# Gate and up projections in other column pieces: 272+272, 512+32, 288+256 per weight block, 384+160

## The chip, the cores and the metric

The kernel runs on one core of a Trainium2 chip. The metric is the device time of one execution, in microseconds (us), as the median of several runs. TensorE is called PE below, its weight loads PEld; DVE is VectorE, ACT ScalarE, POOL GpSimd, SP the engine whose queue starts the weight transfers.

## What is computed

One decoder layer for 512 prompt tokens and 32 sample tokens, 544 in all, with a model width of 1024. A token mixer with three branches (pooling, stick-breaking attention, convolution) is followed by a layer norm and a SwiGLU feed forward, which is the part that matters here:

```python
def _ffn(x, wg, wu, wd):
    return (jax.nn.silu(x @ wg) * (x @ wu)) @ wd
...
xp = _layernorm(ALPHA * xp + _ffn(xp, ffn_w_gate[l], ffn_w_up[l], ffn_w_down[l]), ln2_g[l], ln2_b[l])
```

`wg` and `wu` are 1024 x 2816, `wd` is 2816 x 1024, all float32. Prompt and sample tokens go through the same weights.

## The kernel before, in words

Activations lie with their features on the 128 partitions and the 544 tokens along the free axis: `x1h` and `x1l` are [128, 8, 544], for 8 blocks of 128 features. Matmul operands are in a rounded format (F32R); to come near float32 accuracy each value is split in a high part and a low rest, for activations (`x1h`, `x1l`) and weights (`wh`, `wl`) alike. `gemm` (L212 to L224) then makes one product of three: for each of the 8 feature blocks k it runs wh times x1h, wh times x1l and wl times x1h, which is 24 matmuls into one PSUM bank (a tile of 128x512 float32). The weight block of 128x128 is the stationary operand; the token columns stream past. Every matmul instruction loads its own weights: the trace lists one weight load for each matmul.

The feed forward's first half has NF = 22 blocks f of 128 hidden features. Each has a gate block and an up block of 1024x128 weights. `ffn_half` (L899 to L909) takes one half of the tokens: `HALVES` is columns 0 to 288 (the 32 sample tokens and 256 prompt tokens) and 288 to 544. For a half it runs the gate's 24 matmuls into a bank, Silu on ACT from that bank into `sg` (L905), the up's 24 matmuls into another bank, the product with `sg` on DVE (L908), and the split of the result into `gh` (ACT, L209) and `gl` (DVE, L210). Blocks f = 0 and 1 have their weights ready early and run half by half; blocks 2 to 21 run half 0 and then half 1, so that PE sees gate 288, up 288, gate 256, up 256 columns, 24 matmuls each.

Weights come through `_Weights`: SP's queue brings two blocks of 128 columns at once as `raw`, and `prepare` makes `wh` (ACT, L131) and `wl` (DVE, L132), two blocks ahead, into a pool with three buffers of each. A buffer comes free with the last matmul that reads it. Banks for the results come from a pool of PSM = 5. The tile framework's scheduler places the instructions of each engine; around the change they stand in the order of the code. After the last block the down projection reads `gh` and `gl` as moving operands, in the same two halves.

Of the kernel before, what the change touches and what calls it, by code (L numbers as in the profile page):

```python
# [9 lines left out]
F32 = mybir.dt.float32  # L10
F32R = mybir.dt.float32r
I32 = mybir.dt.int32
AF = mybir.ActivationFunctionType
ALU = mybir.AluOpType
PSUM = bass.MemoryType.PSUM

P = 128
D = 1024
KD = D // P
# [4 lines left out]
T = NP + NS  # L24
# [16 lines left out]
TA = NS + PH  # L41
HALVES = ((0, TA), (TA, T))
# [104 lines left out]
def hybrid_layer_kernel(  # L147
# [6 lines left out]
    nc = tc.nc  # L154
# [13 lines left out]
    def bank(tag="mm"):  # L168
        return pst[tag].tile([P, 512], F32, tag=tag, name=tag)
# [37 lines left out]
    def split_psum(hi, lo, ps, scale=None):  # L207
        if scale is None:
            nc.scalar.copy(hi, ps)  # L209
            nc.vector.tensor_tensor(out=lo, in0=ps, in1=hi.bitcast(F32), op=ALU.subtract)  # L210
        else:
            nc.scalar.mul(hi, ps, scale)  # L212
            nc.vector.scalar_tensor_tensor(out=lo, in0=ps, scalar=scale, in1=hi.bitcast(F32), op0=ALU.mult, op1=ALU.subtract)

    def gemm(ps, wt, rt, kts, c0, c1, wc0=0, first=True, last=True, r0=0, r1_=P):
        n = c1 - c0
        wh, wl = wt
        rh, rl = rt
        steps = [(a, k) for k in range(len(kts)) for a in range(3)]
        for s, (a, k) in enumerate(steps):  # L220
            lw = (wh, wh, wl)[a][r0:r1_, k, wc0:wc0 + P]
            rr = (rh, rl, rh)[a][r0:r1_, kts[k], c0:c1]
            ins = nc.tensor.matmul(ps[:, :n], lw, rr, start=first and s == 0, stop=last and s == len(steps) - 1)  # L223
        return ins  # L224

    # constants
    vt = cp.tile([P, NV], F32, name="vt")
    et = cp.tile([P, NEARLY], F32, name="et")
    ident = et[:, E_ID:E_ID + P]
# [51 lines left out]
    def sqrt_set(ins):  # L281
        with tc.issue_after(ins):
            nc.scalar.preload_act_table_set("sqrt_and_others")
# [2 lines left out]
        with tc.issue_after(ins):  # L286
            nc.scalar.preload_act_table_set("natural_log_exp_and_others")

# [1 line left out]
    nc.gpsimd.memset(qbd, 0.0)  # L290
    nc.gpsimd.memset(osum, 0.0)
    with pool("s0", 1, reuse_waits="tile") as s0:
# [36 lines left out]
        nc.vector.scalar_tensor_tensor(out=pix, in0=pix, scalar=128.0, in1=rwc[:, 0:1].to_broadcast([P, 8 * DB]), op0=ALU.mult, op1=ALU.add)  # L329
        nc.vector.scalar_tensor_tensor(out=piv, in0=piv, scalar=32.0, in1=rwc[:, 1:2].to_broadcast([P, 2 * DB]), op0=ALU.mult, op1=ALU.add)  # L330

# [1 line left out]
    pps = ExitStack()  # L333
    pp = pps.enter_context(pool("pp", reuse_waits="tile"))
    ph_ = pp.tile([P, 2, T], F32R, name="ph")
# [7 lines left out]
    for c in range(2):  # L343
# [8 lines left out]
        n = PB + NP + DB * PEXT  # L352
# [11 lines left out]
        for s in range(2):  # L364
            r = slice(64 * s, 64 * s + 64)
            nc.vector.scalar_tensor_tensor(out=pf[r, NS + PB:], in0=sm[s][r, 2 * PB:PB + NP], scalar=ec_(E_IW + c, 1)[r],
                                           in1=ue[r, 2 * PB:PB + NP], op0=ALU.mult, op1=ALU.subtract)
            nc.vector.scalar_tensor_tensor(out=sview(pf[r, :NS], DS), in0=sview(sm[s][r, PB + NP:], PEXT)[:, :, PB:], scalar=ec_(E_IW + c, 1)[r],
                                           in1=uv[r, :, PB:], op0=ALU.mult, op1=ALU.subtract)
# [5 lines left out]
        nc.gpsimd.dma_start(pool_p[c * P:(c + 1) * P], ue[:, NP:NP + PB])  # L375
        nc.gpsimd.dma_start(pool_s[c * P:(c + 1) * P], fl)

# [1 line left out]
    av = []  # L379
    for c in range(2):  # L380
        a = s1.tile([P, T], F32, tag="av", bufs=2, name=f"av{c}")
# [3 lines left out]
    for c in range(2):  # L385
        sg = s1.tile([P, T], F32, tag="sg", bufs=2, name=f"sg{c}")
# [95 lines left out]
                    nc.vector.tensor_scalar(gt[:, m, c0:c1], ps[:, :c1 - c0], bias, None, op0=ALU.add)  # L482
        return gt, nc.scalar.activation(gt, gt, AF.Sigmoid)

# [1 line left out]
    def gate0(g):  # L486
        gt, ins = gates(0, g, mp_, "gt", GTB)
        for m in range(2):
            nc.vector.tensor_tensor(out=mg[:, 2 * g + m], in0=mg[:, 2 * g + m], in1=gt[:, m], op=ALU.mult)
        return ins  # L490

    pw = w.next()
    for mo in range(KD):
        g, m = mo // 2, mo % 2
        rs = 64 * (g % 2)
        for c0, c1 in HALVES:
            ps = bank("z")
            for n_, (a, b) in enumerate(((pw[0], ph_), (pw[0], pl_), (pw[1], ph_))):
                nc.tensor.matmul(ps[:, :c1 - c0], a[rs:rs + 64, g // 2, m * P:(m + 1) * P], b[rs:rs + 64, g // 2, c0:c1],  # L499
                                 start=n_ == 0, stop=n_ == 2)  # L500
# [4 lines left out]
    for g in range(NGA):  # L505
        ins = gate0(g)

# [1 line left out]
    def qkv_q(ap, hp):  # L509
        qh = ap.tile([P, NP], F32R, tag="qh", name=f"qh{hp}")  # L510
        ql = ap.tile([P, NP], F32R, tag="ql", name=f"ql{hp}")
        for hf, ps in enumerate(chunk_psums(w.next(), X, KX)):
            a = hf * PH
            split_psum(qh[:, a:a + PH], ql[:, a:a + PH], prompt_of(ps, hf), 0.125)
            for s in range(2 if hf == 0 else 0):
                r = slice(64 * s, 64 * s + 64)
                h = 2 * hp + s
                nc.scalar.mul(qbd[r, hp, :, DS * h:DS * h + DS], sview(ps[r, :NS], DS), 0.125)
        return qh, ql
# [89 lines left out]
                exp_set(conv_norm().ins)  # L609
    conv_st.close()  # L610

# [1 line left out]
    sam = ExitStack()  # L613
    sp = sam.enter_context(pool("sam", reuse_waits="tile"))
    g1s = ExitStack()
# [80 lines left out]
    for b in range(DB):  # L696
# [8 lines left out]
        for br, g in [c for c, n_ in zip(steps, at_batch) if n_ == b]:  # L705
# [3 lines left out]
            elif br == 3:  # L709
                cw_ = w.next()  # L710
                for m in range(2):
                    mo = 2 * g + m
                    for c0, c1 in HALVES:
                        ps = bank()
# [16 lines left out]
    cst_.close()  # L731
    s2c.close()

# [1 line left out]
    late = {}  # L735
    for g in range(2):
        w.group(big(w_out, g * 256, 0, KD, 256), KD, 256, ((0, 128), (128, 128)))
# [22 lines left out]
    for g in range(4):  # L760
# [7 lines left out]
        for m, hf in both:  # L768
                mo = 2 * g + m
                c0, c1 = HALVES[hf]  # L770
                ps = bank()
# [8 lines left out]
    pst["mm"] = ctx.enter_context(pool("mm2", PSM, space=PSUM, reuse_waits="tile"))  # L780
    pst["tp"] = ctx.enter_context(pool("tp2", 8 - PSM, space=PSUM, reuse_waits="tile"))

# [1 line left out]
    xp1 = ctx.enter_context(pool("x1", side="right", reuse_waits="tile"))  # L784
    x1h = xp1.tile([P, KD, T], F32R, name="x1h")
    x1l = xp1.tile([P, KD, T], F32R, name="x1l")
# [87 lines left out]
    for m in range(4):  # L874
        wt = w.next()
# [3 lines left out]
    first = [[w.next(), w.next()] for _ in range(2)]  # L879
# [10 lines left out]
    s6t.close()  # L890
    s6.close()

# [1 line left out]
    gp = ctx.enter_context(pool("gp", side="right", reuse_waits="tile"))  # L894
    gh = gp.tile([P, NF, T], F32R, name="gh")
    gl = gp.tile([P, NF, T], F32R, name="gl")
    X1 = (x1h, x1l)
    with pool("s7", 2, reuse_waits="tile") as s7:
        def ffn_half(f, hf, wt, sgs):  # L899
            c0, c1 = HALVES[hf]  # L900
            pg = bank()
            gemm(pg, wt[0], X1, KX, c0, c1)
            n = c1 - c0
            sg = s7.tile([P, TA], F32, tag="sg", bufs=4, name=f"sg{f}{hf}")[:, :n]
            lasts.append(nc.scalar.activation(sg, pg[:, :n], AF.Silu))  # L905
            pu = bank()
            gemm(pu, wt[1], X1, KX, c0, c1)
            nc.vector.tensor_tensor(out=sg, in0=pu[:, :n], in1=sg, op=ALU.mult)  # L908
            split_psum(gh[:, f, c0:c1], gl[:, f, c0:c1], sg)  # L909

        lasts = []
        for hf in range(2):
            for f in range(2):
                ffn_half(f, hf, first[f], None)
        for f in range(2, NF):
            wt = [w.next(), w.next()]
            for hf in range(2):
                ffn_half(f, hf, wt, None)
        sqrt_set(lasts[-1].ins)
    wp2s.close()  # L920

# [26 lines left out]
    for m in range(KD - 1):  # L948
        pss = [bank(), bank()]
        for j, (k0, k) in enumerate(pieces):  # L950
            wt = w.next()
# [124 lines left out]
```

## Time and profile before

| what | value |
|---|---|
| runs | 900.57 and 901.0 us, median 900.79 |
| profiled execution | span of 899.0 us from its first to its last instruction |
| median of the runs less the span | 1.8 us |
| mean granted clock of TensorE | 0.994 of full speed |

Busy times of engines are in the rows below. Matmuls are pipelined, and the duration of one contains its way through the array; what a matmul costs in a row of many is the distance from its start to the next one's, which is called its pitch here.

### The profile page before, as it was taken

Reading aid. Unit: us, or ns where it says so; the run is one execution under the profiler, and the core shown is the slowest. Engines: PE = TensorE matmul, PEld = TensorE weight load, DVE = VectorE, ACT = ScalarE, POOL = GpSimd, SP = SyncE. Lnnn points to the kernel's source line nnn. Section 1 sums busy time; section 2 is a strip of 40 time slices with the busy share of each in tenths; the row PEclk is TensorE's granted clock in tenths of the full one; section 3 lists DMA queues with packets and bytes.
Section 4 is the critical chain, followed back from the end, with each engine's and each line's share of the span. In section 5 each row is a group of like instructions: output and inputs, shape, how many; then the busy total and the mean of one; then the engine's idle time right before and its main releaser. Section 6 shows DMA issues by size and latency. Waiting matters only on the chain.

```text
span 899.0 us, 16259 instructions
## 1 busy us (share of the span) xinstructions
PE 877.0 (98%) x6889; PEld 811.0 (90%) x6889; DVE 478.1 (53%) x845; ACT 348.5 (39%) x583; POOL 134.8 (15%) x158
## 2 busy tenths in 40 slices
PE   7999999999999999999999999999999999999993
PEld 6999999887886667779999999999999999999993
DVE  4899886887343454449646433333333333334437
ACT  5445377776533315244513333232323232222211
POOL 1430100005257476310001000000000000000002
PEclk9999999999999999999999999999999999999997
DMA  9314323214648688646610122233232322323322
GB/s 291 118 34 115 96 73 113 65 38 137 214 143 289 238 290 291 229 136 225 207 48 1 48 68 76 92 95 94 94 95 94 95 58 73 101 75 83 96 81 100
DMA packets 96393, 110.36 MB, mean 123 GB/s; under 512 B 4416, under 2 KB 88224, under 8 KB 94144
## 3 DMA queue, kind: packets, MB, share of 16 engines
q1 hardware_dynamic: 87840, 73.12, 26.4%
q0 software_dynamic: 8480, 36.20, 11.9%
q8 instruction: 54, 0.88, 0.4%
q14 instruction: 19, 0.16, 0.1%
HBM read 104.44 MB, written 4.87 MB: 122 GB/s over the span
## 4 chain that ended last, share of the span: by engine, by line
PE 96%; DVE 2%; ACT 1%; DMA 1%; issue 0%; SPq 0%; another core or an unknown queue 0%; DVEq 0%; ACTq 0%
PE mm L223 82%; PE z L654 3%; PE o L680 2%; PE z L564 2%; PE o L586 2%; PE tp L583 1%; PE tp L795 1%; PE o L681 1%; PE z L499 1%; DMA raw<-in_w_in 1%; PE tp L861 1%; DVE y L999 0%; DVE y L991 0%; PE tp L687 0%; DVE rc L572 0%
## 5 line engine op out<-in xcount | busy, mean ns | idle before, releaser
L132 DVE TENSOR_TENSOR wl<-raw,wh 128x1024 fp32r<-128x1024 f32 (+1 forms) x129 | 152.3, 1184 | 137.7 <-ACT wh L131 136.5
L131 ACT CAST wh<-raw 128x1024 fp32r<-128x1024 f32 (+1 forms) x129 | 129.3, 1006 | 238.9 <-PE mm L223 212.2
L223 PE MATMUL mm<-xh,wh 128*128 128x256 f32 (+1 forms) x672 | 198.3, 295 | 5.7 <-ACT wh L131 5.6
L223 PE MATMUL mm<-x1l,wh 128*128 128x288 f32 (+1 forms) x704 | 202.7, 288 | 0.0
L223 PE MATMUL mm<-x1h,wl 128*128 128x288 f32 (+1 forms) x704 | 201.4, 287 | 0.0
L223 PE MATMUL mm<-x1h,wh 128*128 128x288 f32 (+1 forms) x704 | 200.5, 286 | 0.1
L223 PE MATMUL mm<-xl,wh 128*128 128x256 f32 (+1 forms) x672 | 198.1, 295 | 0.2 <-DVE xl L210 0.2
L223 PE MATMUL mm<-xh,wl 128*128 128x288 f32 (+1 forms) x672 | 197.0, 294 | 0.7 <-issue 0.7
L223 PEld LDWEIGHTS mm<-xh,wh 128*128 128x128 f32 x672 | 127.9, 191 | 16.9 <-issue 9.8
L223 PEld LDWEIGHTS mm<-xl,wh 128*128 128x128 f32 x672 | 127.8, 190 | 8.6 <-issue 7.3
L223 PEld LDWEIGHTS mm<-xh,wl 128*128 128x128 f32 x672 | 127.5, 190 | 8.6 <-issue 7.7
L223 PEld LDWEIGHTS mm<-x1l,wh 128*128 128x128 f32 x704 | 132.2, 188 | 0.2
L223 PEld LDWEIGHTS mm<-x1h,wh 128*128 128x128 f32 x704 | 132.0, 188 | 0.4 <-ACT sg L905 0.3
L223 PEld LDWEIGHTS mm<-x1h,wl 128*128 128x128 f32 x704 | 132.0, 188 | 0.0
L223 PE MATMUL mm<-gl,wh 128*128 128x256 f32 (+1 forms) x352 | 101.7, 289 | 0.0
L223 PE MATMUL mm<-gh,wh 128*128 128x256 f32 (+1 forms) x352 | 101.3, 288 | 0.0
L223 PE MATMUL mm<-gh,wl 128*128 128x256 f32 (+1 forms) x352 | 100.8, 286 | 0.0
L623 POOL DMA_INDIRECT kr<-in_ck,pix x64 | 67.6, 1056 | 44.7 <-PE z L654 20.6
L908 DVE TENSOR_TENSOR sg<-mm,sg 128x288 f32<-128x288 f32 (+1 forms) x44 | 19.4, 441 | 91.8 <-PE mm L223 91.8
L223 PEld LDWEIGHTS mm<-gl,wh 128*128 128x128 f32 x352 | 66.1, 188 | 0.1
L223 PEld LDWEIGHTS mm<-gh,wh 128*128 128x128 f32 x352 | 66.2, 188 | 0.0
L223 PEld LDWEIGHTS mm<-gh,wl 128*128 128x128 f32 x352 | 66.1, 188 | 0.0
(216 smaller groups left out, 1202.8 us busy)
## 6 DMA issues: line engine op xcount, KB each, us to landing
raw<-in_w_in SPq DMA_DIRECT2D x14, 1024.0 KB, 8.2
raw<-in_w_g SPq DMA_DIRECT2D x11, 1024.0 KB, 5.3
raw<-in_w_u SPq DMA_DIRECT2D x11, 1024.0 KB, 5.4
raw<-in_w_d SPq DMA_DIRECT2D x16, 512.0 KB, 4.0
raw<-in_w_in SPq DMA_DIRECT2D x12, 512.0 KB, 3.9
raw<-in_w_out SPq DMA_DIRECT2D x4, 1024.0 KB
raw<-in_w_d SPq DMA_DIRECT2D x8, 384.0 KB, 4.3
raw<-in_w_att_o SPq DMA_DIRECT2D x4, 512.0 KB, 3.4
```

What stands on the lines that cost most here:

```text
L131: self.nc.scalar.copy(hi[:, a:b], v[:, a:b])
L132: self.nc.vector.tensor_tensor(out=lo[:, a:b], in0=v[:, a:b], in1=hi[:, a:b].bitcast(F32), op=ALU.subtract)
L223: ins = nc.tensor.matmul(ps[:, :n], lw, rr, start=first and s == 0, stop=last and s == len(steps) - 1)
L499: nc.tensor.matmul(ps[:, :c1 - c0], a[rs:rs + 64, g // 2, m * P:(m + 1) * P], b[rs:rs + 64, g // 2, c0:c1], start=n_ == 0, stop=n_ == 2)
L564: nc.tensor.matmul(zp[:, :wd], a[r, qs], b[r, :wd], start=n_ == 0, stop=n_ == 2)
L583: nc.tensor.transpose(tp[:, kb], rc[:, s, kb * P:(kb + 1) * P], ident)
L586: nc.tensor.matmul(op_[64 * s:64 * s + 64, :P], vtok[:, kb, 64 * s:64 * s + 64], at[:, kb], start=kb == 0, stop=kb == i)
L623: nc.gpsimd.indirect_dma_start(out=kr[:, u].rearrange("p h c -> p (h c)"), out_offset=None, in_=ck, in_offset=bass.IndirectOffsetOnAxis(ap ...
L654: nc.tensor.matmul(zp[32 * jj:32 * jj + 32, :256], qbd[:, hp, b], kvt[b, "k", jj][:, :, hp], start=hp == 0, stop=hp == 3)
L680: nc.tensor.matmul(op_[32 * c:32 * c + 32], at[:, j], kvt[b, "v", j // 4][:, j % 4], start=j < 4, stop=j >= 4 and c < 3)
L681: nc.tensor.matmul(op_[96:128], at[96:128, 8], vs96[96:128], start=False, stop=True)
L908: nc.vector.tensor_tensor(out=sg, in0=pu[:, :n], in1=sg, op=ALU.mult)
```

## The change

It replaces `ffn_half` by a part with free column bounds, `ffn_part`, and by `ffn_both`, and chooses for each group of five blocks f how the tokens are cut: f = 2 to 6 as 272+272 columns, 7 to 11 as 512+32, 12 to 16 by `ffn_both`, 17 to 21 as 384+160. `ffn_both` keeps the pieces of 288 and 256 columns, but for each weight block k it runs both pieces with wh, each with x1h and x1l, then both with wl, into two banks at a time. Blocks 0 and 1 are as before. The `sg` tiles grow from 288 to 512 columns. The other changed lines of the diff are comments.

```diff
-        def ffn_half(f, hf, wt, sgs):
-            c0, c1 = HALVES[hf]
+        def piece(f, ps, c0, c1, act, sg=None):
+            n = c1 - c0
+            if act:
+                sg = s7.tile([P, 512], F32, tag="sg", bufs=4, name=f"sg{f}{c0}")[:, :n]
+                lasts.append(nc.scalar.activation(sg, ps[:, :n], AF.Silu))
+                return sg
+            nc.vector.tensor_tensor(out=sg, in0=ps[:, :n], in1=sg, op=ALU.mult)
+            split_psum(gh[:, f, c0:c1], gl[:, f, c0:c1], sg)
+
+        def ffn_part(f, cols, wt):
+            c0, c1 = cols
             pg = bank()
             gemm(pg, wt[0], X1, KX, c0, c1)
-            n = c1 - c0
-            sg = s7.tile([P, TA], F32, tag="sg", bufs=4, name=f"sg{f}{hf}")[:, :n]
-            lasts.append(nc.scalar.activation(sg, pg[:, :n], AF.Silu))
+            sg = piece(f, pg, c0, c1, True)
             pu = bank()
             gemm(pu, wt[1], X1, KX, c0, c1)
-            nc.vector.tensor_tensor(out=sg, in0=pu[:, :n], in1=sg, op=ALU.mult)
-            split_psum(gh[:, f, c0:c1], gl[:, f, c0:c1], sg)
+            piece(f, pu, c0, c1, False, sg)
+
+        def ffn_both(f, wt):
+            sg = [None, None]
+            for j in range(2):
+                pss = [bank(), bank()]
+                wh, wl = wt[j]
+                for k in range(KD):
+                    for a, (lw, xs) in enumerate(((wh, (x1h, x1l)), (wl, (x1h,)))):
+                        for ps, (c0, c1) in zip(pss, HALVES):
+                            for x in xs:
+                                nc.tensor.matmul(ps[:, :c1 - c0], lw[:, k], x[:, k, c0:c1], start=k == 0 and a == 0 and x is x1h, stop=k == KD - 1 and a == 1)
+                for hf, (c0, c1) in enumerate(HALVES):
+                    sg[hf] = piece(f, pss[hf], c0, c1, j == 0, sg[hf])
 
         lasts = []
         for hf in range(2):
             for f in range(2):
-                ffn_half(f, hf, first[f], None)
+                ffn_part(f, HALVES[hf], first[f])
+        CUTS = (((0, 272), (272, T)), ((0, 512), (512, T)), None, ((0, 384), (384, T)))
         for f in range(2, NF):
             wt = [w.next(), w.next()]
-            for hf in range(2):
-                ffn_half(f, hf, wt, None)
+            cut = CUTS[(f - 2) // 5]
+            if cut is None:
+                ffn_both(f, wt)
+            else:
+                for cols in cut:
+                    ffn_part(f, cols, wt)
```

On PE, in block f = 7, where the up block's first piece ends and the gate block's second piece begins (`wh` and `wl` with 6245 and 6246 are the up block, with 6241 and 6242 the gate block), there stood before:

```order
L223 MATMUL mm<-x1h,wh_6245 128x288
L223 MATMUL mm<-x1l,wh_6245 128x288
L223 MATMUL mm<-x1h,wl_6246 128x288
L223 MATMUL mm<-x1h,wh_6241 128x256
L223 MATMUL mm<-x1l,wh_6241 128x256
L223 MATMUL mm<-x1h,wl_6242 128x256
```

and now stands:

```order
L223 MATMUL mm<-x1h,wh_6245 128x512
L223 MATMUL mm<-x1l,wh_6245 128x512
L223 MATMUL mm<-x1h,wl_6246 128x512
L223 MATMUL mm<-x1h,wh_6241 128x32
L223 MATMUL mm<-x1l,wh_6241 128x32
L223 MATMUL mm<-x1h,wl_6242 128x32
```

The places of the matmuls and their number are the same; only the columns of each have moved from the second piece to the first. With 384+160 it is the same with other numbers.

On PE, in block f = 12 (the gate block is 6841 and 6842, the up block 6847 and 6848), at the end of the up block's first piece, there stood before:

```order
L223 MATMUL mm<-x1h,wh_6847 128x288
L223 MATMUL mm<-x1l,wh_6847 128x288
L223 MATMUL mm<-x1h,wl_6848 128x288
L223 MATMUL mm<-x1h,wh_6841 128x256
L223 MATMUL mm<-x1l,wh_6841 128x256
L223 MATMUL mm<-x1h,wl_6842 128x256
```

and in this stretch, where the gate block now ends and the up block begins, stands:

```order
L926 MATMUL mm<-x1h,wh_6841 128x288
L926 MATMUL mm<-x1l,wh_6841 128x288
L926 MATMUL mm<-x1h,wh_6841 128x256
L926 MATMUL mm<-x1l,wh_6841 128x256
L926 MATMUL mm<-x1h,wl_6842 128x288
L926 MATMUL mm<-x1h,wl_6842 128x256
L926 MATMUL mm<-x1h,wh_6847 128x288
L926 MATMUL mm<-x1l,wh_6847 128x288
```

The four matmuls that use one `wh` now stand next to each other, and the two that use one `wl`; the gate block is done with after the first half of the matmuls of f, not after three quarters. The rows of ACT, DVE and SP stand in the same order as before, with other widths, except that in blocks 12 to 16 the two pieces' results come one right behind the other.

## Rows read from the trace of the kernel before

**Rows 1.** The page, part 1: busy us, share of the span, number of instructions.

```profile
PE 877.0 (98%) x6889; PEld 811.0 (90%) x6889; DVE 478.1 (53%) x845; ACT 348.5 (39%) x583; POOL 134.8 (15%) x158
```

**Rows 2.** The page, part 4: the chain that ended last, by engine, by line.

```profile
PE 96%; DVE 2%; ACT 1%; DMA 1%; issue 0%; SPq 0%; another core or an unknown queue 0%; DVEq 0%; ACTq 0%
PE mm L223 82%; PE z L654 3%; PE o L680 2%; PE z L564 2%; PE o L586 2%; PE tp L583 1%; PE tp L795 1%; PE o L681 1%; PE z L499 1%; DMA raw<-in_w_in 1%; PE tp L861 1%; DVE y L999 0%; DVE y L991 0%; PE tp L687 0%; DVE rc L572 0%
```

**Rows 3.** Windows of blocks 2 to 21: busy us by engine, clock, DMA.

```profile
core 0: us, PE busy (x) PEld busy (x) DVE busy (x) ACT busy (x) POOL busy (x), PEclk, DMA share, GB/s
510.00:630.00 120.00, 120.00 (x967) 120.00 (x966) 40.38 (x60) 34.72 (x60) 0.00 (x0) 1.00 0.28 88
630.00:748.60 118.60, 118.60 (x956) 118.60 (x955) 41.06 (x60) 35.97 (x61) 0.14 (x2) 1.00 0.27 84
```

**Rows 4.** Timeline of PE in blocks 2 to 21: start us, us, instruction.

```profile
510.10 0.29 PE L223 MATMUL mm<-x1h,wh 128*128 128x288 f32 x1
...
516.32 0.29 PE L223 MATMUL mm<-x1h,wl 128*128 128x288 f32 x1
516.45 0.28 PE L223 MATMUL mm<-x1h,wh 128*128 128x256 f32 x1
...
522.04 0.29 PE L223 MATMUL mm<-x1h,wh 128*128 128x288 f32 x1
...
748.90 0.29 PE L223 MATMUL mm<-gh,wh 128*128 128x288 f32 x1
```

**Rows 5.** Lines by form, 510 to 749 us: count, busy us, mean ns, idle before.

```profile
L223 PEld LDWEIGHTS mm<-x1h,wh 128*128 128x128 f32 x640 | 120.3, 188 | 0.0
L223 PE MATMUL mm<-x1h,wh 128*128 128x288 f32 x320 | 93.8, 293 | 0.0
L223 PE MATMUL mm<-x1h,wh 128*128 128x256 f32 x321 | 89.4, 279 | 0.0
L132 DVE TENSOR_TENSOR wl<-raw,wh 128x1024 fp32r<-128x1024 f32 x39 | 47.8, 1226 | 56.7 <-ACT wh L131 56.7
L131 ACT CAST wh<-raw 128x1024 fp32r<-128x1024 f32 x39 | 40.9, 1049 | 62.9 <-PE mm L223 48.3 <-issue 14.6
```

**Rows 6.** Timeline of PE in the prompt attention (L564), 512 columns.

```profile
213.79 0.40 PE L564 MATMUL z<-kl,qh 64*128 64x512 f32 x1
214.03 0.39 PE L564 MATMUL z<-kh,ql 64*128 64x512 f32 x1
```

**Rows 7.** Timeline in the prompt attention (L564), 128 columns, two heads at once.

```profile
133.96 0.19 PEld L564 LDWEIGHTS z<-kh,qh 64*128 64x128 f32 x2
134.06 0.20 PEld L564 LDWEIGHTS z<-kl,qh 64*128 64x128 f32 x2
134.12 0.28 PE L564 MATMUL z<-kl,qh 64*128 64x128 f32 x2
134.17 0.20 PEld L564 LDWEIGHTS z<-kh,ql 64*128 64x128 f32 x2
134.23 0.28 PE L564 MATMUL z<-kh,ql 64*128 64x128 f32 x2
```

**Rows 8.** Timeline of block 0, behind transposes: first loads of a full weight block.

```profile
482.03 0.19 PEld L223 LDWEIGHTS mm<-x1l,wh 128*128 128x128 f32 x1
482.14 0.19 PEld L223 LDWEIGHTS mm<-x1h,wl 128*128 128x128 f32 x1
482.27 0.30 PE L223 MATMUL mm<-x1h,wl 128*128 128x288 f32 x1
```

**Rows 9.** Windows at the start and the end, columns as in rows 3.

```profile
5.00:10.00 5.00, 4.25 (x13) 3.20 (x14) 3.45 (x6) 2.93 (x6) 0.00 (x0) 1.00 1.06 316
885.00:890.00 5.00, 0.41 (x2) 0.20 (x2) 5.00 (x7) 0.67 (x2) 4.84 (x2) 0.88 0.35 146
890.00:895.00 5.00, 0.00 (x0) 0.00 (x0) 4.83 (x8) 0.00 (x0) 0.00 (x0) 0.50 0.33 117
```

**Rows 10.** Timeline of PE in a gate product: the quickest 256-column stretch looked at.

```profile
266.44 0.28 PE L223 MATMUL mm<-xh,wh 128*128 128x256 f32 x1
...
266.77 0.28 PE L223 MATMUL mm<-xh,wh 128*128 128x256 f32 x1
```

## The prediction

> **What bounds the kernel now.** Start with the busy shares: PE is busy for 877.0 of 899.0 us, and the weight loads beside it for 811.0 [rows 1]. The chain of waits says whether that is the path: 96% of it is PE, 82% the one matmul line that the gate and up products share [rows 2]. In the windows of blocks f = 2 to 21, the stretch that is changed, PE is busy throughout at a granted clock of 1.00, while DVE is busy for 81.4 of 238.6 us and ACT for 70.7 [rows 3]. So the end moves by what a matmul costs PE here, and by nothing else until another engine is three times as busy.
>
> What one costs is its pitch, not its duration of 279 to 293 ns [rows 5]. From the timeline [rows 4]: 48 matmuls of 288 columns take 516.45 - 510.10 = 6.35 us, 132.3 ns each; 48 of 256 take 522.04 - 516.45 = 5.59 us, 116.5 ns each. A pair of pieces, one weight block over all 544 tokens, costs 248.8 ns; and 20 blocks of 48 pairs do take 748.90 - 510.10 = 238.8 us. The pitch goes with the columns: 0.459 and 0.455 ns per column, and 0.24 us for 512, 0.469 with a reading to 10 ns [rows 6]. No fixed part shows at these widths.
>
> Yet there is one under it. Each matmul loads its own weights, 640 loads for the 641 matmuls that use x1h and wh, even where the matmul ahead used the same block [rows 5]. Rows with 128 columns show what that costs once the columns no longer cover it: the loads start at 133.96, 134.06, 134.17, the second and third matmul at 134.12 and 134.23, so the pitch is 0.11 us where 128 columns at 0.459 would be 0.059 [rows 7]. The load sets it: the first matmul streams from 134.06, and the second starts 0.06 later, as 0.459 per column gives, but then waits for its load. These loads have 64 rows; with a full block, behind a stretch of transposes, the second load also starts 0.11 us after the first, and the second matmul 0.13 after that [rows 8], the 288-column pitch. So I take **0.110 us as the least pitch of a matmul with a load of its own**.
>
> **The change, part by part.** Matmuls, loads, casts and DMAs keep their number and, but for blocks 12 to 16, their places; only columns move. A group has 5 blocks x 2 products x 24 = 240 pairs.
>
> *272+272.* Between the two measured pitches 272 gives 124.4 ns, a pair 248.8: no change. At 0.459 per column the pair would be 249.9, +0.3 us for the group. I take 0.
>
> *512+32.* The wide piece costs 512 x 0.4594 = 235.2 ns. The narrow one would be 15 ns by its columns, below the load, so 110. The pair goes from 248.8 to 345.2: 96.4 ns x 240 = **+23.1 us**.
>
> *384+160.* 176.4 ns for the wide piece; the narrow one is 73.5 by its columns, so again 110. The pair: 286.4, 37.6 ns more, x 240 = **+9.0 us**.
>
> *288+256 per weight block.* Matmuls and widths are the same, and so are the loads, since the rows show none left out for a repeated block. The bank now changes four times per k; where it changes now, at 516.32 to 516.45, the step is an ordinary pitch [rows 4]. I take 0. Bounds: the quickest 256-column stretch has (266.77 - 266.44) / 3 = 110 ns [rows 10]; if all matmuls of the group came down in that proportion, 248.8 x 0.056 x 240 = 3.3 us gained. If every change of bank cost as much as a reading could hide, 5 ns, 4 x 8 x 2 x 5 = 320 of them cost 1.6.
>
> *The covers.* A weight block is cast in 1.05 + 1.23 us [rows 5]. With 512+32 the gate's buffer comes free ahead of 24 x 0.110 = 2.6 us of up and 5.6 us of the next gate; with 384+160 ahead of 2.6 + 4.2; by weight block ahead of 6. All exceed 2.3. DVE and ACT get the same columns in other portions, at a third of PE's time. If a cover failed, the next up product would start late, by at most the 2.3 us of one block.
>
> The price of a narrow matmul is the one estimate, since no row has 32 or 160 columns with full weights. From above: if a load had to wait until the stream before it was through, 110 + 15 and 110 + 73.5. From below: columns alone, 15 and 73.5. The nearest rows are those with 128 columns, which lie between the two widths, and there the load overlaps the stream; hence 110.
>
> **Sum**: 899.0 + 23.1 + 9.0 = 931.1 us of span. The runs' median is 1.8 above this span, so **933 us**. With the 256-column pitch of 116.5 as the floor it would be 240 x 2 x 6.5 ns = 3.1 more, with 105 (the reading's lower end) 2.4 less.
>
> **The rivals.**
>
> *Not slower: narrow pieces cost their columns.* If several weight loads can be on the way at once, or PE leaves out what is small, a narrow piece costs 15 and 73.5 ns, and the groups +0.2 and +0.3 us: 901. For it speaks that nowhere in rows 4 does a load show. Against it: 128 columns took 110 ns, not 59 [rows 7]. It decides, in that the sum falls within 2%, from a floor below 80 ns. Chance 0.07. The Trainium skill, "TensorE: Matmul & The Clock Gate", section Back-to-back issue gap, gives about 60 cycles for 1 to 64 columns and 134 for 128, at 2.4 GHz, for single matmuls: estimated from it, a 32-column piece costs 25 ns, a 160-column one about 69, and the kernel takes some 903 us. By that table the 128-column rows would have 56 ns; they have 110.
>
> *Loads don't overlap.* The narrow pieces cost 125 and 183.5 ns: 240 x (0.1114 + 0.1111) = +53 us, 954. For it: with a stream of 32 columns there is hardly anything to overlap with. Against it: at 134.17 the third load starts 0.05 us after the second matmul's, and well ahead of its end [rows 7], and 288 columns and a load take 132 ns together, not 242 [rows 4]. Chance 0.04. The Trainium skill, "TensorE: Matmul & The Clock Gate", section Part 3 (Packing small matmuls), says that a weight load overlaps running matmuls only when it goes to another group of rows; read strictly, this rival would follow from it, and rows 4 contradict it, since there every load fills all rows.
>
> *Narrow matmuls run at a lower rate.* If F32R streams at half rate below some width, 160 columns cost 147 ns, 37 more than the load, +8.9 us, while 32 columns stay under the load: 942. At a quarter, 294 ns, +44 us: 977. Against it: at 128 columns the second matmul started 0.06 us after the first began to stream [rows 7]. But those have 64 rows. Chance 0.07, half for each.
>
> *The clock falls.* In the 32-column stretches PE streams 15 of each 110 ns, for 5.3 us at a time. The granted clock fell to 0.50, that is to 1.2 GHz, once in the trace, after PE had nothing to do at the end; with 13 matmuls in 5 us near the start it stayed 1.00 [rows 9]. If the 512-column matmuls behind ran at half, the five blocks would cost 48 x 0.235 = 11.3 us more each, at most: up to 56 us, 933 to 989. Chance 0.04.
>
> **How the numbers follow.** The forecast, 933, has 0.76, with bounds of 926 to 940 from the terms above. The rivals hold 0.07 (901), 0.04 (954), 0.07 (942 or 977) and 0.04 (up to 989); 0.02 are left for a stall that I don't see. The range is 924 to 954: it leaves out the first rival, the quarter rate and most of the clock's, some 0.16. A difference under 2%, 18 us, is about what a measurement of this kernel can't tell from no change. Faster by more has 0.01, since no term gives over 3.3 us; within 2% has 0.08, the first rival with a little; slower 0.91.
>
> **What the next profile would show.** PE from block 2 to the down projection takes 271 us instead of 238.8. In f = 7 to 11 a block lasts 48 x 0.345 = 16.6 us, in 17 to 21 13.7, in the other two groups 11.9. Starts of 32-column and 160-column matmuls both lie 0.11 us apart, and loads next to each other without a gap. Loads still equal matmuls in number, in the per-block group too, and the granted clock is 1.00 throughout. The prediction is wrong if 32 columns take clearly less than 0.1, if 160 columns take longer than 32, or if the per-block group moves by more than 3 us.

## The result and the profile after

The changed kernel takes 944.58 us (944.54 and 944.61) against 900.79: 1.0482 times as long, 95% interval 1.0451 to 1.0512. The profiled execution's span is 942.8 us, 43.8 more than before. The forecast was 933, with 924 to 954 for the range: the way and the main prices held, and 11.5 us came from a rival that had been given a chance of 0.04.

PE is the path as before. The page after, part 1, answers to [rows 1], and the first line of part 4, the chain that ended last, to [rows 2]:

```profile
PE 920.0 (98%) x6889; PEld 841.8 (89%) x6889; DVE 477.3 (51%) x845; ACT 347.4 (37%) x583; POOL 136.1 (14%) x158
PE 96%; DMA 1%; DVE 1%; ACT 0%; issue 0%; SPq 0%; another core or an unknown queue 0%; POOL 0%; DVEq 0%; ACTq 0%
```

The same 6889 matmuls and as many loads keep PE busy 43.0 us longer, while the other engines do what they did. The four groups of blocks, f = 2 to 6, 7 to 11, 12 to 16, 17 to 21, each in a window (busy us by engine, granted clock, DMA, as in [rows 3]):

```profile
510.77:571.00 60.23, 60.23 (x482) 60.23 (x481) 19.47 (x29) 16.70 (x29) 0.00 (x0) 1.00 0.27 87
571.00:662.45 91.45, 91.45 (x483) 79.36 (x481) 21.15 (x30) 17.83 (x30) 0.00 (x0) 0.89 0.19 58
662.45:724.24 61.79, 61.79 (x483) 61.79 (x482) 18.53 (x28) 16.10 (x30) 0.00 (x0) 0.97 0.31 97
724.24:792.65 68.41, 68.41 (x482) 68.41 (x481) 21.57 (x32) 19.34 (x32) 0.14 (x2) 1.00 0.19 58
```

Five blocks took 59.7 us before (238.8 / 4). So the groups cost 0.5, 31.75, 2.1 and 8.7 us more, 43.1 together; the rest of the span is as before, within 0.8. And the clock's column (the third number from the end) shows what was not in the sum: 0.89 in the group with 512+32, 0.97 in the one behind it.

The floor of a narrow matmul first. The timeline of PE and its loads, where block 7 goes from 512 to 32 columns (start us, us, instruction), and then the next change of shape:

```profile
582.04 0.18 PE L223 MATMUL mm<-x1h,wh 128*128 128x32 f32 x1
582.05 0.19 PEld L223 LDWEIGHTS mm<-x1l,wh 128*128 128x128 f32 x1
582.07 0.26 PE L223 MATMUL mm<-x1l,wh 128*128 128x32 f32 x1
582.16 0.19 PEld L223 LDWEIGHTS mm<-x1h,wl 128*128 128x128 f32 x1
582.18 0.26 PE L223 MATMUL mm<-x1h,wl 128*128 128x32 f32 x1
582.27 0.19 PEld L223 LDWEIGHTS mm<-x1h,wh 128*128 128x128 f32 x1
...
587.32 0.75 PE L223 MATMUL mm<-x1h,wh 128*128 128x512 f32 x1
```

Loads stand 0.11 us apart, back to back, and matmuls with them: 48 in 587.32 - 582.04 = 5.28 us, 110 ns each. The shape with five times the columns, in block 17:

```profile
732.58 0.23 PE L223 MATMUL mm<-x1h,wh 128*128 128x160 f32 x1
732.59 0.19 PEld L223 LDWEIGHTS mm<-x1l,wh 128*128 128x128 f32 x1
732.65 0.28 PE L223 MATMUL mm<-x1l,wh 128*128 128x160 f32 x1
732.69 0.19 PEld L223 LDWEIGHTS mm<-x1h,wl 128*128 128x128 f32 x1
732.77 0.27 PE L223 MATMUL mm<-x1h,wl 128*128 128x160 f32 x1
```

The pitch is the same, 0.11 us (5.32 / 48 = 110.8 ns over the whole piece). The second matmul is listed 0.07 us after the first, about the time of 160 columns, and the third 0.12 after that, with its load: read so, the array is free early and waits for the load.

Then the clock. Windows of the first blocks with 512+32, and of the first block behind the group (same columns, the clock third from the end):

```profile
580.00:585.00 5.00, 5.00 (x38) 4.62 (x36) 1.38 (x2) 0.86 (x2) 0.00 (x0) 1.00 0.00 0
585.00:590.00 5.00, 5.00 (x30) 4.45 (x29) 2.61 (x4) 2.07 (x4) 0.00 (x0) 0.74 0.01 2
...
605.00:610.00 5.00, 5.00 (x15) 4.22 (x16) 1.57 (x4) 1.17 (x2) 0.00 (x0) 0.50 0.69 211
...
660.00:665.00 5.00, 5.00 (x35) 5.00 (x35) 2.75 (x4) 2.20 (x4) 0.00 (x0) 0.75 0.00 0
```

PE counts as busy in all of them; the clock is down at the end of a stretch of narrow matmuls and in the wide ones behind it. The timeline where the second such stretch ends shows both levels' price:

```profile
605.60 0.33 PEld L223 LDWEIGHTS mm<-x1l,wh 128*128 128x128 f32 x1
605.67 0.37 PE L223 MATMUL mm<-x1l,wh 128*128 128x32 f32 x1
605.82 0.33 PEld L223 LDWEIGHTS mm<-x1h,wl 128*128 128x128 f32 x1
605.88 0.37 PE L223 MATMUL mm<-x1h,wl 128*128 128x32 f32 x1
606.03 0.33 PEld L223 LDWEIGHTS mm<-x1h,wh 128*128 128x128 f32 x1
606.10 0.77 PE L223 MATMUL mm<-x1h,wh 128*128 128x512 f32 x1
...
606.67 0.63 PE L223 MATMUL mm<-x1l,wh 128*128 128x512 f32 x1
...
607.10 0.63 PE L223 MATMUL mm<-x1h,wl 128*128 128x512 f32 x1
```

At 0.50, that is 1.2 GHz, loads stand 0.21 to 0.22 us apart instead of 0.11, and 512 columns take 0.43 instead of 0.230. Piece by piece the five wide ones of the group last 11.04, 12.70, 13.50, 12.71 and 13.50 us, and the narrow ones 5.28, 6.08, 5.27, 6.09 and 5.28. Only the first wide piece ran at full clock throughout. Against 5 x (11.04 + 5.28) the group lost 91.45 - 81.6 = 9.9 us to the clock, and the first block behind it lasts 13.66 us where its followers take 12.03: 1.6 more. That is the 11.5. The stretches of 160 columns are as long as those of 32 and load as often, and the group with them has a clock of 1.00.

### The profile page after: what moved, and what is told of

Its sections match the earlier page's. It is cut to its first block, busy times and chain, and to the rows that moved or that the text cites. A ratio compares the mean times of both kernels' runs of the same rounds, so it can differ in the third digit from the quotient of the medians.

```text
span 942.8 us, 16264 instructions
## 1 busy us (share of the span) xinstructions
PE 920.0 (98%) x6889; PEld 841.8 (89%) x6889; DVE 477.3 (51%) x845; ACT 347.4 (37%) x583; POOL 136.1 (14%) x158
## 4 chain that ended last, share of the span: by engine, by line
PE 96%; DMA 1%; DVE 1%; ACT 0%; issue 0%; SPq 0%; another core or an unknown queue 0%; POOL 0%; DVEq 0%; ACTq 0%
PE mm L223 77%; PE mm L926 7%; PE z L654 2%; PE o L680 2%; PE z L564 2%; PE o L586 2%; PE tp L583 1%; PE tp L795 1%; PE o L681 1%; PE z L499 1%; DMA kr<-in_ck,pix 1%; DMA raw<-in_w_in 1%; PE tp L861 0%; DVE y L1023 0%; DVE y L1015 0%
## 5 line engine op out<-in xcount | busy, mean ns | idle before, releaser
L223 PE MATMUL mm<-x1l,wh 128*128 128x272 f32 (+6 forms) x544 | 169.9, 313 | 0.0
L223 PE MATMUL mm<-x1h,wh 128*128 128x272 f32 (+6 forms) x544 | 168.7, 312 | 0.1
L223 PE MATMUL mm<-x1h,wl 128*128 128x272 f32 (+6 forms) x544 | 168.8, 311 | 0.0
L223 PEld LDWEIGHTS mm<-x1l,wh 128*128 128x128 f32 x544 | 105.6, 194 | 4.3
L223 PEld LDWEIGHTS mm<-x1h,wl 128*128 128x128 f32 x544 | 105.7, 194 | 4.0
L223 PEld LDWEIGHTS mm<-x1h,wh 128*128 128x128 f32 x544 | 105.3, 194 | 4.3 <-ACT sg L903 0.3
L905 DVE TENSOR_TENSOR sg<-mm,sg 128x272 f32<-128x272 f32 (+6 forms) x44 | 18.9, 440 | 131.9 <-PE mm L223 112.6
```

Source lines behind the costliest of these rows:

```text
L905: nc.vector.tensor_tensor(out=sg, in0=ps[:, :n], in1=sg, op=ALU.mult)
```

## The experiments

Times of before are those of the same chip: 897.08 us beside the first four, 897.31 beside the last three. The changed kernel was not run again beside them, so it is compared by its ratio to before. Diffs are against the changed kernel; lines left out are marked with dots.

**Wide and narrow in turn, matmul by matmul.** In blocks 7 to 11 only:

```diff
+        def ffn_alt(f, cut, wt):
...
+                for k in range(KD):
+                    for a, (lw, x) in enumerate(((wh, x1h), (wh, x1l), (wl, x1h))):
+                        for ps, (c0, c1) in zip(pss, cut):
+                            nc.tensor.matmul(ps[:, :c1 - c0], lw[:, k], x[:, k, c0:c1], start=k == 0 and a == 0, stop=k == KD - 1 and a == 2)
...
+            elif cut[0][1] == 512:
+                ffn_alt(f, cut, wt)
```

> The changed kernel, but in blocks 7 to 11 the 512-column and the 32-column matmul of one weight block stand next to each other, so that the same 480 loads and matmuls no longer come as 5.3 us stretches of narrow ones. Theory (a load is the floor of a narrow matmul, and the fall of the clock cost 11.5 us): a pair still takes 0.230 + 0.110 = 0.340 us, 16.3 us per block, but the granted clock stays 1.00: about 933 us. Rival 1, the slow wide pieces of 0.265 and 0.281 us come from something else than the clock, such as weights arriving: unchanged, 944. Rival 2, a load that is covered by a wide matmul costs nothing on either side: a pair takes 0.245, the blocks 11.8 us each: about 910.

930.82 us, 1.0385 times before (1.0368 to 1.0402), where the changed kernel had 1.0482. A window over nearly all of the five blocks, and in the timeline the first matmul of block 7 and of block 12 (x2 is a wide and a narrow one together):

```profile
570.00:651.00 81.00, 81.00 (x472) 70.54 (x472) 17.62 (x28) 16.48 (x29) 0.00 (x0) 1.00 0.17 57
```

```profile
567.08 0.40 PE L925 MATMUL mm<-x1h,wh 128*128 128x512 f32 x2
...
649.91 0.38 PE L938 MATMUL mm<-x1h,wh 128*128 128x288 f32 x1
```

The five blocks take 82.83 us, 16.6 each and 345.1 ns for a pair of 512 and 32, at a clock of 1.00: the 230 of the wide one, the 110 of a load, and 5 ns. So the theory's two halves stand apart: with the same matmuls and loads, only mixed, the clock stays up and about 1% of the time comes back, while the price of the narrow ones' loads stays. Rival 2, 245 ns a pair, falls: a wide matmul covers one load, and not the next as well. Rival 1 falls too: the slow wide pieces were the clock's.

**Gate 512, gate 32, up 512, up 32.** In blocks 7 to 11 only, the narrow stretches half as long:

```diff
+        def ffn_turn(f, cut, wt):
...
+            for j in range(2):
+                for i, (c0, c1) in enumerate(cut):
+                    ps = bank()
+                    gemm(ps, wt[j], X1, KX, c0, c1)
+                    sg[i] = piece(f, ps, c0, c1, j == 0, sg[i])
...
+            elif cut[0][1] == 512:
+                ffn_turn(f, cut, wt)
```

> The changed kernel, but in blocks 7 to 11 the pieces run as gate 512, gate 32, up 512, up 32, so that the narrow stretches are half as long, 24 matmuls of 0.110 us, 2.6 us. If the length of the stretch decides the clock's fall, it stays at 1.00 and the time is 933 us; if only the share of columns over the whole block decides, it falls as before and the time is 944. The narrow pitch is 0.110 us in both.

939.97 us, 1.0481 times before (1.0463 to 1.0498), against 1.0482 for the changed kernel: nothing regained that is clear of the noise. Windows:

```profile
575.00:580.00 5.00, 5.00 (x17) 3.96 (x16) 1.23 (x1) 0.21 (x2) 0.00 (x0) 0.67 0.00 0
580.00:585.00 5.00, 5.00 (x36) 4.58 (x35) 1.57 (x3) 1.47 (x2) 0.00 (x0) 1.00 0.01 2
590.00:595.00 5.00, 5.00 (x26) 4.42 (x26) 1.23 (x1) 1.29 (x3) 0.00 (x0) 0.69 0.16 54
```

A narrow stretch takes 2.60 us at full clock (24 x 108 ns), but of the ten wide pieces between, which would be 5.52 us each, seven take 7.14 to 7.21. So the clock falls with narrow stretches of half the length too, and costs about as much; when it falls, these runs don't say, beyond that mixing each narrow matmul with a wide one avoided it.

**Half a weight block per load.** In blocks 7 to 11 the 32-column pieces are computed in two halves of 64 hidden features each, in a bank of their own, the second half moved to its partitions by ACT:

```diff
+        def gemm64(ps, wt, r, c0, c1):
+            wh, wl = wt
+            steps = [(lw, x, k) for k in KX for lw, x in ((wh, x1h), (wh, x1l), (wl, x1h))]
+            for s, (lw, x, k) in enumerate(steps):
+                nc.tensor.matmul(ps[:64, :c1 - c0], lw[:, k, r:r + 64], x[:, k, c0:c1], start=s == 0, stop=s == len(steps) - 1)
...
+                    (ffn_narrow if cols[1] - cols[0] == 32 else ffn_part)(f, cols, wt)
```

> The changed kernel, but in blocks 7 to 11 each 32-column piece is computed with weight blocks of 64 columns instead of 128, twice as many matmuls and loads. Theory (the load is the floor and goes with the weight columns): a half load takes about 0.055 us, 96 of them 5.3 us as 48 whole ones did, and the time stays near 944 us, within 5. Rival (the floor of 0.110 us is a price of each matmul, whatever it loads): 96 x 0.110 = 10.6 us per block, 26 us more, about 971.

942.99 us, 1.0514 times before (1.0493 to 1.0535). Timeline:

```profile
582.30 0.21 PE L921 MATMUL mm<-x1l,wh 128*64 128x32 f32 x1
582.33 0.14 PEld L921 LDWEIGHTS mm<-x1h,wl 128*64 128x64 f32 x1
582.36 0.21 PE L921 MATMUL mm<-x1h,wl 128*64 128x32 f32 x1
582.38 0.14 PEld L921 LDWEIGHTS mm<-x1h,wh 128*64 128x64 f32 x1
```

Half a block loads in about half the time: 96 matmuls took 5.57 us where the clock was full, 58 ns each. The floor is the load, and goes with the weight's columns; a price per matmul would have cost 26 us.

**All blocks as 352+192, and all as 304+240.** One line is changed in each; with 304+240 it has 304 in place of 352:

```diff
-        CUTS = (((0, 272), (272, T)), ((0, 512), (512, T)), None, ((0, 384), (384, T)))
+        CUTS = (((0, 352), (352, T)),) * 4
```

> All blocks 2 to 21 as 352+192 columns, piece after piece. Theory (a flat floor of 0.110 us below some 240 columns): 352 columns take 0.160 us, 192 take 0.110, the pair 0.270 against 0.2488, x 960 = 20 us more than before, about 921. Rival 1 (a lower rate for narrow matmuls, 0.69 ns per column as the 160-column ones have): 192 columns take 0.133, 43 us more, 943. Rival 2 (columns alone): 902.

919.47 us, 1.0248 times before (1.0231 to 1.0265), 22.4 us. Starts of the first 192-column matmul of a block and of the next block's first matmul:

```profile
514.25 0.25 PE L223 MATMUL mm<-x1h,wh 128*128 128x192 f32 x1
...
519.59 0.34 PE L223 MATMUL mm<-x1h,wh 128*128 128x352 f32 x1
```

48 of them in 5.34 us are 111.3 ns each: as much as 32 or 160 columns, not 133. A wide one took 160.1. The pair is 271.4 ns, 22.6 more than 248.8, and 960 of these are 21.7 us.

> All blocks 2 to 21 as 304+240 columns. A flat floor of 0.110 us meets the cost of the columns at about 240. Theory: 304 columns take 0.139 us and 240 take 0.111, the pair 0.250 to 0.251 against 0.2488: 1 to 2 us more than before. Rival (matmuls of fewer than 256 columns run at a lower rate): the 240-column ones take longer than the 256-column ones' 0.1165 us, and the kernel is slower by 4 us or more.

900.41 us, 1.0028 times before (1.0017 to 1.0039), 2.5 us. The same two starts:

```profile
525.46 0.27 PE L223 MATMUL mm<-x1h,wh 128*128 128x240 f32 x1
...
530.85 0.31 PE L223 MATMUL mm<-x1h,wh 128*128 128x304 f32 x1
```

5.39 us for 48, or 112.3 ns for 240 columns, less than the 116.5 of 256, so at 240 there is no lower rate; a 304-column one takes 139.2, the pair 251.5 and 2.6 us in all.

**All blocks per weight block, and all as 272+272.** `CUTS = (None,) * 4` and `CUTS = (((0, 272), (272, T)),) * 4`.

> All blocks 2 to 21 per weight block, 288 and 256 columns. In the changed kernel the five such blocks took 2.1 us more than before, but the first of them began at the low clock. Theory (only that first block was slow, the order itself costs 0.09 us per block, 12.03 against 11.94): 20 blocks take 1.8 us more than before, under 0.3%. Rival (the change of bank within a weight block costs the 2.1 us): four times as much, 8 us, 0.9%. Second rival (weights in a row save loads): faster than before by some us.

898.77 us, 1.0017 times before (1.0008 to 1.0026), 1.5 us. A block takes 12.03 us here. So of the 2.1 us that this group cost in the changed kernel, 0.09 a block were the order's, and the rest was the clock's, which was 0.75 where the group began; and having the matmuls of one weight block in a row saved nothing.

> All blocks 2 to 21 as 272+272 columns. In the changed kernel the five such blocks took 60.23 us against 59.7, 0.251 us per pair against 0.2488. If that is the price of these widths, 20 blocks take 2.1 us more than before, 0.24%. If it was a chance of that run, no difference.

898.93 us, 1.0018 times before (1.0009 to 1.0027), 1.6 us. A block takes 12.05 us, as in the changed kernel; before the change it took 11.94. No cut that was tried is faster than the one before.

## Why the prediction came out as it did

*The floor of a narrow matmul: right.* It was taken as 110 ns from rows with 128 columns and 64 rows of weights [rows 7]; measured 110.0 with 32 columns, 110.8 with 160, 111.3 with 192, and shown to be the load. The rivals that rested on it (columns alone, loads that don't overlap, a lower rate) are all out: 160 columns take neither 73.5 nor 183.5 nor 147 ns, and the pitch is flat from 32 to 192 columns.

*384+160: +9.0 forecast, +8.7 measured.* Right, with 174.3 ns for the wide piece where the same price per column gave 176.4.

*512+32: +23.1 forecast, +31.75 measured.* At full clock it is 5 x 16.32 - 59.7 = +21.9, the 512-column piece taking 230.0 and not 235.2 ns. The other 9.9 us are the clock.

*The clock: this is the step that failed.* I set it aside with a chance of 0.04 and expected 1.00 throughout, because the clock had fallen once, with PE idle, and had stayed at 1.00 with 13 matmuls in 5 us [rows 9]. The second reason was a misreading. The clock's column has 1.00 in that window, but the timeline of the kernel before, inside the window and behind it, does not fit that:

```profile
8.70 0.44 PE L223 MATMUL mm<-xh,wh 128*128 128x288 f32 x1
8.70 0.33 PEld L223 LDWEIGHTS mm<-xl,wh 128*128 128x128 f32 x1
8.94 0.44 PE L223 MATMUL mm<-xl,wh 128*128 128x288 f32 x1
...
15.26 0.29 PE L223 MATMUL mm<-xh,wh 128*128 128x288 f32 x1
15.39 0.29 PE L223 MATMUL mm<-xl,wh 128*128 128x288 f32 x1
```

In the changed kernel, where its granted clock is 0.50 (662.50 to 665.50):

```profile
663.96 0.44 PE L926 MATMUL mm<-x1h,wh 128*128 128x288 f32 x1
664.20 0.44 PE L926 MATMUL mm<-x1l,wh 128*128 128x288 f32 x1
```

At 8.70 matmuls of 288 columns stand 0.24 us apart and a load lasts 0.33, as in the changed kernel at 0.50; from 15.26 on the distance is 0.13. So by its matmuls PE was at the low level during those 13, and the row was no evidence against the rival. Nor did they stand behind dense matmuls, as the narrow stretches here do. The rival was priced, but as one thing or nothing, 0 or up to 56 us; it came in part: each wide piece behind a narrow stretch was slow at its beginning and lost 1.7 or 2.5 us by it, and two of the narrow stretches lost 0.8 each. The mixed order, which takes this away, has 1.0385 for 1.0482.

*Per weight block: 0 forecast, +2.1 measured*, of which 1.6 is the same clock, low as the group begins, and 0.09 a block the order. *272+272: 0 forecast, +0.5 measured*, 125.5 ns a matmul where its neighbours' mean is 124.4 and the price per column, the dearer of the two estimates, gave 125.0.

*What was luck.* Without the clock the sum's other misses, -1.2 us for 512+32, -0.3 for 384+160, +0.5 twice in the groups taken as 0 and +0.7 in the rest of the span, nearly cancel. And 944.58 lies inside 924 to 954 although the range was said to leave out most of the clock's rival: its top, 954, is the time that the rival of loads that don't overlap would have given.

*The covers held.* PE is busy for the whole of the four windows, no other engine is on the chain in these blocks, and DVE's and ACT's wider portions show nowhere.

By the Trainium skill, "TensorE: Matmul & The Clock Gate", section Back-to-back issue gap, the time was estimated at 903; the trace does not agree, with 110 ns for 32 columns where that estimate had 25, and the section itself says that its table is for single matmuls and has no weight load in it. The rule of the Trainium skill, "TensorE: Matmul & The Clock Gate", section Part 3 (Packing small matmuls), that a load overlaps running matmuls only when it goes to another group of rows, went with the rival of 954. With 512 and 32 in turn the pair takes 345 ns, 230 and little more than one load, not 230 + 15 + two loads, so the trace does not agree with that rule either.

## What to carry to other kernels

Where every matmul loads its own weights, a matmul costs the larger of its columns and its load; here any piece under some 240 columns is charged like 240, so a remainder should be spread over the pieces and not cut off. If a narrow piece can't be avoided, run its matmuls between wide ones rather than in a stretch of their own: here that did not save the load, but it kept the clock. And where a change makes PE's work sparse, price the clock in parts, by the stretch behind as well as the sparse one, even if the trace before shows no such fall; and check a clock that the profile lists against the pitch of its matmuls.

## What the runs showed of the hardware that was not expected

The granted clock fell although PE counted as busy, its loads ran back to back, and the narrow stretches were as short as 2.6 us. Stretches of 160 columns, with as many loads, left it at 1.00. The load follows the clock: 0.11 us at the full one, 0.21 to 0.22 at half.

A matmul's pitch is not quite in proportion to its columns: at full clock 512 take 230.0 ns, 384 174.3, 352 160.1, 304 139.2, 288 132.3, 272 125.5, 256 116.5, 240 112.3. From 352 to 512 that is 0.437 ns per column over some 6 ns that each matmul pays; 256 lies a little below that line, 272 on it. So equal pieces of 272 cost 2.2 ns a pair more than 288 and 256.
